# Two of the four parts of a state space's input weights formed in turned layout from tables, in place of 32 transposes

## The chip, the cores and the metric

One core of a Trainium2 chip runs the kernel. The metric is the device time of one execution in microseconds. The kernel before takes 1587.14 us, the median of three runs (1587.11 to 1588.02).

## What is computed

The reference is one layer of an encoder over two sequences of 512 tokens and width 1024, each with a memory of 256 rows, in float32. Three branches read the normalized input: a diagonal complex state space (32 groups of 16 channels, 64 states a group, run forwards and backwards), differential attention, and cross attention to the memory. Their outputs are gated, added and projected, and a feed-forward block follows. Cut to what the change touches:

```
h = rmsnorm(x) @ w_in;  u, q, k, v, xq, g = split(h)
mk, mv = split(rmsnorm(mem) @ w_mem_kv)          # keys and values of the memory
lam_bar = exp(lam * step)
b_bar = ((lam_bar - 1) / lam)[..., None] * b     # per group: 64 states x 16 channels
bu = einsum('lgh,gph->lgp', u, b_bar)
xs = scan(x_l = lam_bar * x_{l-1} + bu_l)        # once forwards, once backwards
y = real(einsum('lgp,ghp->lgh', xs, c))
```

## The kernel before

Eight tokens make a chunk. Within a chunk the state that u adds is a product with "input weights": for a group of 16 channels, a table of (8 tokens x 16 channels) by (2 directions x 64 states), real and imaginary, whose entry is lam_bar to a power q that depends on the token, times gamma = (lam_bar - 1) / lam, times b. The names: `pr`, `pi` are the powers of lam_bar (real, imaginary), `qr`, `qi` those in the tokens' order for the input, `xr_`, `xi_` for the output, `gr`, `gi` gamma, `b_r`, `b_i` b times gamma, `l8r`, `l8i` the eighth power for the scan. The 32 groups go in four parts `o` of eight.

`input_weights(o)` forms, for each part, two tables with states on the partitions (`cxr`, `cxi`, L1602 to L1611: six products or sums of 128x1024 on the vector engine, DVE). The matmul that uses them wants tokens and channels on the partitions, so TensorE (PE) turns each 128x128 piece (L1623), eight pieces to a table, and the scalar engine (ACT) copies them from PSUM to `wb` (L1624). The first three parts are formed ahead (L1628), the fourth later (L1693). L1687 multiplies `u_`, the projected input read back from DRAM in chunks (L1674), with `wb`.

All of this is a generator, `s5_gen`. The main function advances it at fixed places between the work on the memory, the input projection and the gates. There the rest of the code runs thus: a weight is loaded to `wf` on the SyncE queue (SP, L146), cast to `wh` on ACT (L134), and the rest `wl` is formed on DVE (L135); `wf`, `wh`, `wl` have two buffers each. The memory's values are four accumulating calls `mem_v(0)` to `mem_v(3)`, with the weights w_mv[0] to w_mv[3]; the four PSUM banks that they fill are emptied by ACT copies to `mf` (L368) and sent to DRAM (L373). The input projection follows, with w_in[0] and w_in[1] first, in the same four banks. `x_norm` (L252 to L254) makes the normalized input, `xh` and `xl`, in the same time, with a factor that PE turns into rows (L69 `rs`).

Each engine works through its own list in order. A scheduler sets the lists when the kernel is built, from its own view of times and the given ties (`issue_after`, `keep_in_program_order`); every instruction waits for its operands and buffers by semaphores. All loads named here are on SP's queue, which is in order as well, and the code of the generator shares the engines with everything else: an instruction that has to wait holds up what stands behind it on its engine.

Of the kernel before, what the change touches and what calls it, by code (L numbers as in the profile page):

```python
# [10 lines left out]
F32 = mybir.dt.float32  # L11
# [3 lines left out]
ALU = mybir.AluOpType  # L15
# [4 lines left out]
P = 128  # L20
# [11 lines left out]
G = 32  # L32
# [1435 lines left out]
def s5_gen(k):  # L1468

    tc, nc, a, slot, aux, drp, ident = k.tc, k.nc, k.a, k.slot, k.aux, k.drp, k.ident  # L1470
    V, S, PO, PE = nc.vector, nc.scalar, nc.gpsimd, nc.tensor
# [3 lines left out]
    cp = rt.enter_context(tc.tile_pool(name="s5c", bufs=1, side="right", reuse_waits="tile"))  # L1475
# [9 lines left out]
    def sm(nm, n=G):  # L1485
        return pp.tile([P, n], F32, tag="m_" + nm, name=nm)
# [40 lines left out]
    pr = pp.tile([P, 9, G], F32, name="pr")  # L1527
    pi = pp.tile([P, 9, G], F32, name="pi")
# [15 lines left out]
    ta, tb = (pp.tile([P, 512], F32, name=n_) for n_ in ("ta", "tb"))  # L1544
    t84a = ta[:, : 8 * G].rearrange("p (e g) -> p e g", g=G)
    t84b = tb[:, : 8 * G].rearrange("p (e g) -> p e g", g=G)
# [6 lines left out]
    mr, gr, gi, dn = sm("mr"), sm("gr"), sm("gi"), sm("dn")  # L1553
# [8 lines left out]
    V.tensor_tensor(out=gr, in0=gr, in1=dn, op=ALU.mult)  # L1562
    V.tensor_tensor(out=gi, in0=gi, in1=dn, op=ALU.mult)

    yield
    br, bi = pp.tile([P, G, 16], F32, name="br"), pp.tile([P, G, 16], F32, name="bi")
    cr, cn = cp.tile([P, G, 16], F32, name="cr"), cp.tile([P, G, 16], F32, name="cn")
    nc.sync.dma_start(br, a["b_re"])
# [8 lines left out]
    cmul(V, b_r, b_i, br, bi, gr.unsqueeze(2).broadcast_to(bs), gi.unsqueeze(2).broadcast_to(bs),  # L1577
         ta.rearrange("p (g h) -> p g h", h=16), tb.rearrange("p (g h) -> p g h", h=16))

    qr, qi = cp.tile([P, 8, G], F32, name="qr"), cp.tile([P, 8, G], F32, name="qi")  # L1580
    xr_, xi_ = cp.tile([P, 8, G], F32, name="xr_"), cp.tile([P, 8, G], F32, name="xi_")
    for (q_, x_, s_) in ((qr, xr_, pr), (qi, xi_, pi)):
        S.copy(q_[0:64], s_[0:64, 7::-1, :])
        S.copy(q_[64:128], s_[64:128, 0:8, :])
        S.copy(x_[0:64], s_[0:64, 1:9, :])
        S.copy(x_[64:128], s_[64:128, 8:0:-1, :])
    l8r = sp.tile([P, 2, G, NS], F32, name="l8r")
# [8 lines left out]
    def by_group(v, o):  # L1596
        return v[:, 8 * o : 8 * o + 8, :].unsqueeze(2).broadcast_to(sh4)

    def by_token(v, o):
        return v[:, :, 8 * o : 8 * o + 8].rearrange("p e g -> p g e").unsqueeze(3).broadcast_to(sh4)  # L1600

    def cprod(tag, ar, ai, xr, xi, sub):  # L1602


        tiles = [slot(tag, [P, 8, 8 if sub else 9, 16], name=n_) for n_ in ("cxr", "cxi")]
        for o_, x1, x2, op in ((tiles[0], ar, ai, ALU.subtract if sub else ALU.add), (tiles[1], ai, ar, ALU.add if sub else ALU.subtract)):
            o_ = o_[:, :, 0:8, :]
            t1 = slot(tag, sh4, name="ct1")
            V.tensor_tensor(out=t1, in0=x1, in1=xr, op=ALU.mult)
            V.tensor_tensor(out=o_, in0=x2, in1=xi, op=ALU.mult)  # L1610
            V.tensor_tensor(out=o_, in0=t1, in1=o_, op=op)  # L1611
        return tiles


    def input_weights(o):
        res = []
        for w_ in cprod("it", by_group(b_r, o), by_group(b_i, o), by_token(qr, o), by_token(qi, o), True):
            w_ = w_.rearrange("p g e h -> p (g e h)")
            t_ = slot("wb", [P, 8 * P], name="wb")
            for g4 in range(2):  # L1620
                tr = aux()
                for g in range(4):
                    PE.transpose(tr[:, g * P : (g + 1) * P], w_[:, (4 * g4 + g) * P : (4 * g4 + g + 1) * P], ident)  # L1623
                S.copy(t_[:, g4 * 512 : g4 * 512 + 512], tr)  # L1624
            res.append(t_)
        return res

    wbs = [input_weights(o) for o in range(3)]  # L1628
    yield

    gD = drp.tile([G, 16, 15, 16], F32, name="gD5")
    cD = drp.tile([4, 2, P, 8, 144], F32, name="cD")
# [5 lines left out]
    def output_weights(o):  # L1638
        Orf, Onf = cprod("it", by_group(cr, o), by_group(cn, o), by_token(xr_, o), by_token(xi_, o), False)
        PO.tensor_copy(Orf[:, :, 8, :], cr[:, 8 * o : 8 * o + 8, :])  # L1640
        PO.tensor_copy(Onf[:, :, 8, :], cn[:, 8 * o : 8 * o + 8, :])
        Orf, Onf = (o_.rearrange("p g e h -> p g (e h)") for o_ in (Orf, Onf))
        nc.sync.dma_start(cD[o, 0], Orf)
        nc.sync.dma_start(cD[o, 1], Onf)
        hs = slice(8 * o, 8 * o + 8)
        for ri, s_ in enumerate((b_r, b_i)):
            S.copy(l48[0:64, ri, :, 0:16], s_[0:64, hs, :])
            S.copy(l48[64:128, ri, :, 16:32], s_[64:128, hs, :])
            S.copy(l48[:, ri, :, 32:48], s_[:, hs, :])
        kps = [aux() for _ in range(2)]  # L1650
        for g4, kp in enumerate(kps):
            for g in range(2):
                for ri, o_ in ((1, Onf), (0, Orf)):
                    for hf in range(2):
                        tc.keep_in_program_order(
                            PE.matmul(kp[64 * hf : 64 * hf + 48, g * 144 : (g + 1) * 144], l48[:, ri, 4 * g4 + 2 * hf + g, :],
                                      o_[:, 4 * g4 + 2 * hf + g, :], start=(ri == 1), stop=(ri == 0)))
        for g4, kp in enumerate(kps):
            gk = cp.tile([112, 2, 144], F32, tag="gk", name="gk", bufs=2)
            for hf in range(2):  # L1660
                r0 = 64 * hf
                S.copy(gk[r0 : r0 + 48].rearrange("p g c -> p (g c)"), kp[r0 : r0 + 48, : 2 * 144])
                gv = gD[8 * o + 4 * g4 + 2 * hf : 8 * o + 4 * g4 + 2 * hf + 2].rearrange("g h t q -> h g (t q)")
                nc.sync.dma_start(gv[:, :, 128:240], gk[r0 : r0 + 16, :, 0:112])
                nc.sync.dma_start(gv[:, :, 0:112], gk[r0 + 16 : r0 + 32, :, 16:128])
                nc.sync.dma_start(gv[:, :, 112:128], gk[r0 + 32 : r0 + 48, :, 128:144])

    output_weights(0)
    output_weights(1)
    uv = k.uD.rearrange("(g h) j s c -> j h g (s c)", h=16)  # L1670
    u_ = slot("su", [P, G, NS * NC], name="u_")
# [27 lines left out]
    for i in range(2, NC):  # L1699
        p_ = sp.tile([P, 2, G * NS], F32, tag="p_", name="p_")  # L1700
        q_ = sp.tile([P, 2, G * NS], F32, tag="q_", name="q_")
# [29 lines left out]
    for o in range(4):  # L1731
# [4 lines left out]
        x2 = slot("x2", [P, 2, 8 * NS, NC], name="x2")  # L1736
# [24 lines left out]
def _tok(x):  # L1761

    return x.reshape(NC, T, *x.shape[1:]).swapaxes(0, 1).reshape(L, *x.shape[1:])
# [30 lines left out]
def layout(i):  # L1794
    i = {k_: np.asarray(v_) for k_, v_ in i.items()}
    a = {}
    x = np.stack([_tok(i["x_prompt"][0]), _tok(i["x_sample"][0])])
    a["xT"] = x.reshape(NS, L, KD, P).transpose(0, 3, 2, 1)
    mem = np.concatenate([i["mem_prompt"][0], i["mem_sample"][0]])
    a["xN"] = x.reshape(NS, 4, P, DM)  # L1800
    a["memN"] = mem.reshape(4, P, DM)
    a["memT"] = mem.reshape(2 * NMEM, KD, P).transpose(2, 1, 0)
    w = i["w_in"][0]
    a["w_in"] = _mtiles(w)
    a["w_v"] = np.stack([_moving(w[:, 1536 + 256 * h : 1792 + 256 * h], 4) for h in range(2)])
    wk = i["w_mem_kv"][0]
    a["w_mk"] = _mtiles(wk[:, :512])
    a["w_mv"] = _moving(wk[:, 512:], 2)
    a["w_glu"] = _mtiles(i["s5_w_glu"][0])
    a["w_up"] = np.stack([_mtiles(i["w_up"][0, n]) for n in range(3)])  # L1810
    a["w_out"] = _mtiles(i["w_out"][0])
    a["w_fg"] = _mtiles(i["w_ffn_in"][0][:, :FF])
    a["w_fu"] = _mtiles(i["w_ffn_in"][0][:, FF:])
    a["w_fo"] = _mtiles(i["w_ffn_out"][0])
    vecs = {"norm_mix": i["norm_mix"][0], "norm_mem": i["norm_mem"][0], "norm_ffn": i["norm_ffn"][0],
            "norm_final": i["norm_final"], "s5_d": i["s5_d"][0], "s5_b_glu": i["s5_b_glu"][0],
            "diff_subln": i["diff_subln"][0]}
    a["vecs"] = np.concatenate([_cols(vecs[n]) for n in VEC], axis=1)
    a["ident"] = np.eye(P, dtype=np.float32)
    a.update(_rope())  # L1820
    lam = np.stack([i["diff_lambda_q1"][0], i["diff_lambda_q2"][0], i["diff_lambda_k1"][0], i["diff_lambda_k2"][0]])
    a["lamv"] = np.broadcast_to(lam[None], (P, 4, 64))
    dpg = lambda v: v.transpose(0, 2, 1).reshape(P, G)
    a["lam_re"] = dpg(i["s5_lambda_re"][0])
    a["lam_im"] = dpg(i["s5_lambda_im"][0])
    a["log_step"] = dpg(np.broadcast_to(i["s5_log_step"][0][:, :, None], (2, G, 64)))
    for nm in ("re", "im"):
        b = i["s5_b_" + nm][0]
        a["b_" + nm] = b.transpose(0, 2, 1, 3).reshape(P, G, 16)
        c = i["s5_c_" + nm][0]  # L1830
        a["c_" + nm] = c.transpose(0, 3, 1, 2).reshape(P, G, 16)
    return {k_: np.ascontiguousarray(v_, dtype=np.float32) for k_, v_ in a.items()}
# [20 lines left out]
```

## Time and profile before

| What | us |
|---|---|
| median of three runs | 1587.14 |
| the profiled execution | 1586.94 |
| its span, first to last instruction | 1585.2 |
| PE busy (7738 matmuls and transposes) | 1574.0 |
| DVE busy | 1170.4 |
| ACT busy | 631.6 |
| all waits of PE for other engines | 5.1 |
| the 64 transposes of L1623 lie between | 74 and 131 |

A row of a timeline in the profile has the start in us, the length, the engine, the line and operation, what is written and read with partitions x elements, a count of like instructions, and in brackets the idle time before with what ended it. Matmuls are pipelined: a row's length is longer than the distance to the next. Rows of the view of one line have the shortest, median and longest duration in ns.

### The profile page before, as it was taken

The numbers are of one execution on the slowest core, as the hardware profiler recorded it, in microseconds if no ns is written. First come the engines' busy times: TensorE is split into PE (matmuls) and PEld (weight loads), VectorE is DVE, ScalarE is ACT, GpSimd is POOL, SyncE is SP. The second block draws the span as 40 slices with busy tenths as digits, with TensorE's granted clock in tenths as the row PEclk, the third lists the DMA queues.
The fourth block names the chain that finished last, engine by engine and source line by source line (L and its number), as shares of the span: only waits on it lengthen the run. The fifth ranks groups of instructions, "written<-read, shape, count | busy, mean of one in ns | idle before, by whom it ended". The sixth has DMA issues, their size and how long they took to land. (4 is left out here: it accounts for less than half of the span.)

```text
span 1585.2 us, 21351 instructions
## 1 busy us (share of the span) xinstructions
PE 1574.0 (99%) x7738; PEld 1310.4 (83%) x7738; DVE 1170.4 (74%) x1859; ACT 631.6 (40%) x1115; POOL 549.5 (35%) x434
## 2 busy tenths in 40 slices
PE   9999999999999999999999999999999999999998
PEld 7888888888898779778888888888888888888777
DVE  7978995076774776866545669788888877988864
ACT  6644223265552455564223443333333333233323
POOL 0010000001333321300343355767777553444663
PEclk9999999999999999999999999999999999999999
DMA  9553623676763121135544422333333323885412
GB/s 363 183 170 119 212 94 116 180 266 204 269 218 113 41 100 41 47 127 174 198 140 128 137 93 93 112 107 120 120 120 125 118 84 128 306 324 184 160 61 107
DMA packets 105675, 237.84 MB, mean 150 GB/s; under 512 B 13665, under 2 KB 45409, under 8 KB 105569
## 3 DMA queue, kind: packets, MB, share of 16 engines
q1 hardware_dynamic: 104992, 236.06, 44.2%
q8 instruction: 61, 1.00, 0.3%
q14 instruction: 46, 0.37, 0.1%
q10 hardware_dynamic: 576, 0.41, 0.1%
HBM read 165.16 MB, written 71.27 MB: 149 GB/s over the span
## 5 line engine op out<-in xcount | busy, mean ns | idle before, releaser
L66 PE MATMUL bkmm<-xh,wh 128*128 128x512 f32 x640 | 255.3, 399 | 0.0
L66 PE MATMUL bkmm<-xh,wl 128*128 128x512 f32 x640 | 250.6, 392 | 0.0
L66 PE MATMUL bkmm<-xl,wh 128*128 128x512 f32 x640 | 250.1, 391 | 0.0
L66 PE MATMUL bkmm<-tl,wh 128*128 128x512 f32 (+1 forms) x621 | 241.1, 388 | 0.0
L66 PE MATMUL bkmm<-th,wl 128*128 128x512 f32 (+1 forms) x621 | 240.7, 388 | 0.0
L66 PE MATMUL bkmm<-th,wh 128*128 128x512 f32 (+1 forms) x621 | 240.7, 388 | 0.0
L134 ACT CAST wh<-wf 128x1024 fp32r<-128x1024 f32 (+2 forms) x134 | 117.6, 878 | 261.2 <-PE bkmm L66 190.4
L135 DVE TENSOR_TENSOR wl<-wf,wh 128x1024 fp32r<-128x1024 f32 (+2 forms) x134 | 147.6, 1102 | 60.5 <-ACT wh L134 55.4
L66 PE MATMUL bkmm<-th,w 128*128 128x512 f32 x432 | 140.7, 391 | 1.9 <-DVE nsq L1112 1.2
L66 PEld LDWEIGHTS bkmm<-xh,wh 128*128 128x128 f32 x640 | 120.3, 188 | 26.2 <-issue 3.4
L66 PEld LDWEIGHTS bkmm<-xh,wl 128*128 128x128 f32 x640 | 120.2, 188 | 26.2 <-issue 0.4
L66 PEld LDWEIGHTS bkmm<-xl,wh 128*128 128x128 f32 x640 | 120.4, 188 | 22.3
L66 PEld LDWEIGHTS bkmm<-th,wh 128*128 128x128 f32 x621 | 116.6, 188 | 24.0
L66 PEld LDWEIGHTS bkmm<-th,wl 128*128 128x128 f32 x621 | 116.5, 188 | 24.1 <-DVE wl L135 0.2
L66 PEld LDWEIGHTS bkmm<-tl,wh 128*128 128x128 f32 x621 | 116.6, 188 | 23.8
L1175 POOL TENSOR_TENSOR up<-up,acc 128x512 f32<-128x512 f32 x44 | 83.7, 1920 | 90.6 <-DVE up L1112 86.8
L452 POOL TENSOR_TENSOR raw<-raw 128x128 f32<-128x128 f32 x28 | 14.6, 523 | 288.9 <-DVE nb L543 231.9
L66 PEld LDWEIGHTS bkmm<-th,w 128*128 128x128 f32 x432 | 80.9, 188 | 22.1 <-DVE nsq L1112 2.1
L792 POOL TENSOR_TENSOR mg<-mg,gl 128x1024 f32<-128x1024 f32 x16 | 43.8, 2740 | 136.8 <-DVE gl L788 132.1
L66 PE MATMUL bkmm<-tl,w 128*128 128x512 f32 x216 | 84.1, 389 | 0.0
L134 ACT CAST wh<-ws 128x1024 fp32r<-128x1024 f32 x44 | 46.3, 1052 | 91.3 <-PE bkmm L66 49.7
L66 PE MATMUL bkmm<-yh,wh 128*128 128x512 f32 x192 | 76.2, 397 | 0.0
(663 smaller groups left out, 3535.4 us busy)
## 6 DMA issues: line engine op xcount, KB each, us to landing
wf<-in_w_in SPq DMA_DIRECT2D x40, 512.0 KB, 3.9
wD<-hl SPq DMA_DIRECT2D x28, 512.0 KB, 2.9
w<-wD SPq DMA_DIRECT2D x28, 512.0 KB, 4.8
gD<-gt SPq DMA_DIRECT2D x24, 512.0 KB, 2.9
gl<-gD SPq DMA_DIRECT2D x24, 512.0 KB, 3.7
wf<-in_w_fg SPq DMA_DIRECT2D x22, 512.0 KB, 3.6
wf<-in_w_fu SPq DMA_DIRECT2D x22, 512.0 KB, 3.5
aD<-ac SPq DMA_DIRECT2D x22, 512.0 KB, 2.8
```

Of the source, the lines that this page charges most:

```text
L66: return self.put(self.eng.matmul(*args, **kw))
L134: h = S.copy(hi, src)
L135: l_ = V.tensor_tensor(out=lo, in0=src, in1=hi.bitcast(F32), op=ALU.subtract)
L452: PO.tensor_tensor(out=a22, in0=a21, in1=a22, op=ALU.add)
L792: PO.tensor_tensor(out=mg[m], in0=mg[m], in1=gt, op=ALU.add)
L1175: PO.tensor_tensor(out=up, in0=up, in1=accs[s], op=ALU.mult)
```

## The change

For parts 1 and 2 (the second and third) the input weights are formed with tokens and channels on the partitions at once. Tables in that layout are needed for both factors:

- The power times gamma, `qgr` and `qgi`, is formed for the 16 groups of both parts by six small DVE instructions (128x8x16, in the new code after L1563), in the scratch tiles `ta` and `tb`. PE turns both (two transposes, L1577), ACT copies them from PSUM back into `ta` (L1579), and two DMAs write them to DRAM as `qD` (L1581). The four ACT copies that make `qr` and `qi` move ahead to this place; before, they stood with those of `xr_` and `xi_` behind b times gamma.
- b in turned layout, `bt_re` and `bt_im`, comes as two new inputs, laid out on the host.
- `tables_in(o)` loads four tables of 128x1024 for a part: two of b (512 KB each, L1644) and two of the power, each by eight DMAs that read one row of 4 KB of `qD` into 16 partitions (L1647). They use four of the five slots `mem` that the memory's work holds until `mem_v` is through.
- `turned_weights` multiplies them by six DVE instructions of 128x1024 a part (L1656 to L1658), whose result is `wb` itself.

Part 1 stands with part 0, part 2 behind `output_weights(0)`. Parts 0 and 3 are as before. So 32 of the 64 transposes and eight of the 16 ACT copies go, two transposes, one ACT copy, six small DVE instructions and 38 DMAs come.

```diff
--- before.py
+++ after.py
@@ -1562,7 +1562,23 @@
     V.tensor_tensor(out=gr, in0=gr, in1=dn, op=ALU.mult)
     V.tensor_tensor(out=gi, in0=gi, in1=dn, op=ALU.mult)
 
+    qr, qi = cp.tile([P, 8, G], F32, name="qr"), cp.tile([P, 8, G], F32, name="qi")
+    for (q_, s_) in ((qr, pr), (qi, pi)):
+        S.copy(q_[0:64], s_[0:64, 7::-1, :])
+        S.copy(q_[64:128], s_[64:128, 0:8, :])
+    qgr, qgi = (t_[:, 8 * G : 12 * G].rearrange("p (e g) -> p e g", e=8) for t_ in (ta, tb))
+    qs_, mid = [P, 8, 16], slice(8, 24)
+    cmul(V, qgr, qgi, qr[:, :, mid], qi[:, :, mid], gr[:, mid].unsqueeze(1).broadcast_to(qs_),
+         gi[:, mid].unsqueeze(1).broadcast_to(qs_), t84a[:, :, :16], t84b[:, :, :16])
     yield
+    qD = drp.tile([2, 8, 16, P], F32, name="qD")
+    tr = aux()
+    for ri, q_ in enumerate((qgr, qgi)):
+        PE.transpose(tr[:, ri * P : (ri + 1) * P], q_.rearrange("p e g -> p (e g)"), ident)
+    qt = ta[:, : 2 * P].rearrange("p (a n) -> p a n", n=P)
+    S.copy(qt.rearrange("p a n -> p (a n)"), tr[:, : 2 * P])
+    for ri in range(2):
+        nc.sync.dma_start(qD[ri].rearrange("e g n -> (e g) n"), qt[:, ri])
     br, bi = pp.tile([P, G, 16], F32, name="br"), pp.tile([P, G, 16], F32, name="bi")
     cr, cn = cp.tile([P, G, 16], F32, name="cr"), cp.tile([P, G, 16], F32, name="cn")
     nc.sync.dma_start(br, a["b_re"])
@@ -1577,11 +1593,8 @@
     cmul(V, b_r, b_i, br, bi, gr.unsqueeze(2).broadcast_to(bs), gi.unsqueeze(2).broadcast_to(bs),
          ta.rearrange("p (g h) -> p g h", h=16), tb.rearrange("p (g h) -> p g h", h=16))
 
-    qr, qi = cp.tile([P, 8, G], F32, name="qr"), cp.tile([P, 8, G], F32, name="qi")
     xr_, xi_ = cp.tile([P, 8, G], F32, name="xr_"), cp.tile([P, 8, G], F32, name="xi_")
-    for (q_, x_, s_) in ((qr, xr_, pr), (qi, xi_, pi)):
-        S.copy(q_[0:64], s_[0:64, 7::-1, :])
-        S.copy(q_[64:128], s_[64:128, 0:8, :])
+    for (x_, s_) in ((xr_, pr), (xi_, pi)):
         S.copy(x_[0:64], s_[0:64, 1:9, :])
         S.copy(x_[64:128], s_[64:128, 8:0:-1, :])
     l8r = sp.tile([P, 2, G, NS], F32, name="l8r")
@@ -1625,8 +1638,29 @@
             res.append(t_)
         return res
 
-    wbs = [input_weights(o) for o in range(3)]
-    yield
+    def tables_in(o):
+        tabs = [slot("mem", [P, 8 * P], name="tab") for _ in range(4)]
+        for t_, nm in zip(tabs[2:], ("bt_re", "bt_im")):
+            nc.sync.dma_start(t_, a[nm][:, 8 * P * o : 8 * P * (o + 1)])
+        for ri, t_ in enumerate(tabs[:2]):
+            for e in range(8):
+                nc.sync.dma_start(t_[16 * e : 16 * e + 16],
+                                  qD[ri, e, 8 * o - 8 : 8 * o].rearrange("g n -> (g n)").unsqueeze(0).broadcast_to([16, 8 * P]))
+        return tabs
+
+    def turned_weights(q_r, q_i, bt_r, bt_i):
+        res = []
+        for x1, x2, op in ((bt_r, bt_i, ALU.subtract), (bt_i, bt_r, ALU.add)):
+            t_ = slot("wb", [P, 8 * P], name="wb")
+            t1 = slot("it", [P, 8, 9, 16], name="ct1").rearrange("p g e h -> p (g e h)")[:, : 8 * P]
+            V.tensor_tensor(out=t1, in0=x1, in1=q_r, op=ALU.mult)
+            V.tensor_tensor(out=t_, in0=x2, in1=q_i, op=ALU.mult)
+            V.tensor_tensor(out=t_, in0=t1, in1=t_, op=op)
+            res.append(t_)
+        return res
+
+    tab = tables_in(1)
+    wbs = [input_weights(0), turned_weights(*tab)]
 
     gD = drp.tile([G, 16, 15, 16], F32, name="gD5")
     cD = drp.tile([4, 2, P, 8, 144], F32, name="cD")
@@ -1666,6 +1700,9 @@
                 nc.sync.dma_start(gv[:, :, 112:128], gk[r0 + 32 : r0 + 48, :, 128:144])
 
     output_weights(0)
+    tab = tables_in(2)
+    wbs.append(turned_weights(*tab))
+    yield
     output_weights(1)
     uv = k.uD.rearrange("(g h) j s c -> j h g (s c)", h=16)
     u_ = slot("su", [P, G, NS * NC], name="u_")
@@ -1826,6 +1863,8 @@
     a["log_step"] = dpg(np.broadcast_to(i["s5_log_step"][0][:, :, None], (2, G, 64)))
     for nm in ("re", "im"):
         b = i["s5_b_" + nm][0]
+        bt = b.transpose(3, 1, 0, 2).reshape(1, 16, G * P)
+        a["bt_" + nm] = np.broadcast_to(bt, (8, 16, G * P)).reshape(P, G * P)
         a["b_" + nm] = b.transpose(0, 2, 1, 3).reshape(P, G, 16)
         c = i["s5_c_" + nm][0]
         a["c_" + nm] = c.transpose(0, 3, 1, 2).reshape(P, G, 16)
```

The lists of the engines change so. Lines are those of each kernel, so the same code has other numbers behind the new lines (L1585 before is L1598 after); `xt_147` and `xt_148` are first tiles of the two sequences' input, `wh<-wf` is the cast of a weight.

The first place is ACT from the last `xh` of the first sequence on; the three casts of weights there are w_mv[3], w_in[0] and w_in[1], in this order. Before:

```order
L253 CAST xh_130<-xt_147 128x512
L134 CAST wh<-wf 128x1024
L253 CAST xh_123<-xt_148 128x512
L253 CAST xh_124<-xt_148 128x512
L134 CAST wh<-wf 128x1024
L253 CAST xh_125<-xt_149 128x512
L253 CAST xh_126<-xt_149 128x512
L368 COPY mf<-bkmm 128x512 x2
L253 CAST xh_127<-xt_150 128x512
L134 CAST wh<-wf 128x1024
L1583 COPY qr<-pr 64x256
```

With the change, from the same row:

```order
L253 CAST xh_130<-xt_147 128x512
L1579 COPY ta<-bktr 128x256
L134 CAST wh<-wf 128x1024
L253 CAST xh_123<-xt_148 128x512
L253 CAST xh_124<-xt_148 128x512
L134 CAST wh<-wf 128x1024
L253 CAST xh_125<-xt_149 128x512
L253 CAST xh_126<-xt_149 128x512
L253 CAST xh_127<-xt_150 128x512
L134 CAST wh<-wf 128x1024
```

The copy of the new transposes has come in ahead of the cast of w_mv[3], and the two `mf` copies are no longer ahead of the cast of w_in[1]. They stand further down; these are the rows of the change from that cast on:

```order
L134 CAST wh<-wf 128x1024
L1598 COPY xr__735<-pr 64x256
L1599 COPY xr__735<-pr 64x256
L1598 COPY xi__736<-pi 64x256
L1599 COPY xi__736<-pi 64x256
L1604 COPY l8r<-pr 128x32 x2
L1605 ACTIVATE l8i<-pi 128x32
L368 COPY mf<-bkmm 128x512
L1606 COPY l8i<-pi 128x32
```

The first `mf` copy has moved behind the cast of w_in[1], four copies of `xr_` and `xi_` and three of the eighth power.

The second place is PE between `mem_v(2)` and `mem_v(3)` (`mh_142` and `ml_146` are the memory's tiles of `mem_v(3)`), as a piece of the difference:

```order
 L66 MATMUL bkmm<-wl,mh_141 128x512 x8
 L69 MATMUL bktr<-ident,rs 128x128 x4
+L1577 MATMUL bktr<-ident,ta 128x128
+L1577 MATMUL bktr<-ident,tb 128x128
 L66 MATMUL bkmm<-wh,mh_142 128x512 x2
 L66 MATMUL bkmm<-wh,ml_146 128x512 x2
```

The two new transposes stand directly ahead of `mem_v(3)`.

The third place is ACT some 25 rows earlier, in the first sequence's `xh` (the cast of a weight between is w_mv[1]). Before:

```order
L253 CAST xh_124<-xt_147 128x512
L134 CAST wh<-wf 128x1024
L238 ACTIVATE tk,ss<-tk 128x1024 x2
L253 CAST xh_125<-xt_147 128x512
L134 CAST wh<-wf 128x1024
```

With the change:

```order
L253 CAST xh_124<-xt_147 128x512
L1567 COPY qr<-pr 64x256
L1568 COPY qr<-pr 64x256
L134 CAST wh<-wf 128x1024
L1567 COPY qi<-pi 64x256
L1568 COPY qi<-pi 64x256
L238 ACTIVATE tk,ss<-tk 128x1024 x2
L253 CAST xh_125<-xt_147 128x512
L134 CAST wh<-wf 128x1024
```

The copies that make `qr` stand ahead of the cast of w_mv[1] now, those of `qi` ahead of the cast of w_mv[2].

## The prediction

> **What bounds the kernel now.** I read the page first: the span and the busy times.
>
> ```profile
> span 1585.2 us, 21351 instructions
> PE 1574.0 (99%) x7738; PEld 1310.4 (83%) x7738; DVE 1170.4 (74%) x1859; ACT 631.6 (40%) x1115; POOL 549.5 (35%) x434
> ```
>
> PE is busy in 99% of the span, every other engine far less. Then the waits of PE, by what ended them; I show the three longest.
>
> ```profile
> PE bkmm L66 <- DVE nsq L1112: 1.2, 2, 0.6
> PE bktr L66 <- DVE pad_r L82: 1.2, 1, 1.2
> PE bktr L66 <- ACT nsq L1417: 0.7, 1, 0.7
> ```
>
> All seven rows of that view come to 5.1 us. So the time is PE's own work, one instruction behind the other, and two rules follow. Work taken from PE shortens the span by its length. Whatever makes PE wait lengthens it by the whole wait, because there is no later idle time to swallow it. Work of DVE, ACT or the DMA queue counts only where PE comes to stand behind it. The places to look at are the 32 transposes that go, and the stretch from 34 to 60 us, where the change puts new instructions ahead of some on which PE waits.
>
> **Removed: 32 transposes, -3.54 us.** The line view of L1623, then PE's timeline around one group of eight.
>
> ```profile
> L1623 PE MATMUL bktr<-ident,cxr x32: 270/272/273, 74.3 to 126.9; 128*128 128x128 f32 x32
> L1623 PE MATMUL bktr<-ident,cxi x32: 272/272/273, 77.3 to 131.0; 128*128 128x128 f32 x32
> ```
> ```profile
> 74.08 0.40 PE L66 MATMUL bkmm<-xl,wh 128*128 128x512 f32 x1
> 74.32 1.03 PE L1623 MATMUL bktr<-ident,cxr 128*128 128x128 f32 x8
> 75.11 0.48 PE L66 MATMUL bkmm<-xh,wl 128*128 128x512 f32 x1
> 75.43 0.39 PE L66 MATMUL bkmm<-xh,wh 128*128 128x512 f32 x1
> 75.66 0.40 PE L66 MATMUL bkmm<-xl,wh 128*128 128x512 f32 x1
> ```
>
> The 272 ns of one is a duration in a pipeline, not its price. From the start of the group to the second matmul behind it are 75.43 - 74.32 = 1.11 us; without the group this holds one 128x512 matmul, whose pitch is 75.66 - 75.43 = 0.23. A group costs 0.88 to 0.89, and four groups go: 4 x 0.886 = **3.54 us**. The least that one could argue is the eight starts alone, 75.11 - 74.32 = 0.79, or 3.16. The eight ACT copies of L1624 that go as well free an engine at 40%: nothing.
>
> DVE forms as many 128x1024 products as before (six for each part), and six small ones more; that is weighed below.
>
> **Added ahead of the memory values' last weights: +2.03 us by the time PE starts on them.** Here are PE and ACT in the stretch where the order has changed (the order's rows are shown above).
>
> ```profile
> 36.38 1.98 PE L66 MATMUL bkmm<-wh,mh 128*128 128x512 f32 x8
> ...
> 47.37 0.60 PE L69 MATMUL bktr<-ident,rs 128*128 128x128 f32 x4
> 47.72 0.71 PE L66 MATMUL bkmm<-wh,mh 128*128 128x512 f32 x2
> ...
> 53.35 0.39 PE L66 MATMUL bkmm<-xh,wh 128*128 128x512 f32 x1
> ```
> ```profile
> 34.74 1.05 ACT L134 CAST wh<-wf 128x1024 fp32r<-128x1024 f32 x1
> ...
> 43.91 1.05 ACT L134 CAST wh<-wf 128x1024 fp32r<-128x1024 f32 x1
> ...
> 52.19 1.08 ACT L368 COPY mf<-bkmm 128x512 f32<-128x512 f32 x2
> ...
> 53.67 1.06 ACT L134 CAST wh<-wf 128x1024 fp32r<-128x1024 f32 x1
> 54.63 0.41 ACT L1583 COPY qr<-pr 64x256 f32<-64x256 f32 x1
> 55.04 0.40 ACT L1584 COPY qr<-pr 64x256 f32<-64x256 f32 x1
> ...
> 59.08 0.34 ACT L1591 COPY l8r<-pr 128x32 f32<-128x32 f32 x2
> 59.33 0.62 ACT L253 CAST xh<-xt 128x512 fp32r<-128x512 f32 x1
> 59.85 0.23 ACT L1592 ACTIVATE l8i<-pi 128x32 f32<-128x32 f32 x1
> 59.98 0.60 ACT L253 CAST xh<-xt 128x512 fp32r<-128x512 f32 x1
> ```
>
> First, the two qr copies now precede the cast at 34.74. They have starts 0.41 apart, and an ACT instruction of another kind starts some 0.1 before the end of the last, so two of them cost about 0.73. The cast ends 36.52 instead of 35.79; PE began at 36.38: **+0.2**.
>
> Second, DVE must finish six more small products before PE's two new transposes. This is its row of the nearest size and the subtraction (wl) that stands behind these products.
>
> ```profile
> 34.13 0.29 DVE L1541 TENSOR_TENSOR tb<-pi,pr 128x128 f32<-128x128 f32 x1
> 34.45 0.29 DVE L1542 TENSOR_TENSOR pi<-ta,tb 128x128 f32<-128x128 f32 x1
> ...
> 46.34 1.23 DVE L135 TENSOR_TENSOR wl<-wf,wh 128x1024 fp32r<-128x1024 f32 x1
> ```
>
> Six by 0.21 to 0.32 is 1.3 to 1.9; I take 1.3, as most of these are not in a chain with the one before. DVE waits 0.73 longer for the late cast, but does 0.4 of small work in that wait which it did later before. So tb is ready at 46.34 + 0.33 + 1.3 = 48.0. PE gets there at 47.37 + 0.2 + 4 x 0.0875 (the four L69 starts, 0.35 in all) + 0.09 = 48.0. I take 0.05 for this wait; its ends are 0 and 0.6.
>
> Third, and this is the step that costs: the ACT copy of these transposes now stands in ACT's order **ahead of the cast of the fourth memory-value weight** (43.91 above), and ACT works in order. That cast was done at 44.96, with 47.72 - 44.96 = 2.76 to spare. Now it waits for PE: transposes done at 48.05 + 0.27 = 48.3, copy of 128x256 about 0.4 (the trace has 0.40 for 64x256 and half of the 1.08 row, 0.54, for 128x512: those are the ends), cast 1.05, done at 49.75. PE, which must have it next, starts at 49.75 and not 47.72: **+2.03**, of which 1.6 is this wait and 0.2 the transposes themselves.
>
> **What that pushes: +3.16 more.** The subtraction that was at 46.34 follows the late cast, 49.75 to 50.98. It frees the raw weight buffer for the second input-projection weight, whose load SP issues then.
>
> ```profile
> 47.59 0.33 SPq L146 DMA_DIRECT2D wf<-in_w_in  x1
> ```
> ```profile
> DMA to landing us min/median/max: 3.9/3.9/3.9
> ```
>
> (The second view is L146 in that moment alone.) Before: issued 47.59, landed 51.5. After: issued 51.0, landed 54.9. ACT's order has the cast of that weight next (54.9 to 55.95), and then, unlike before, the four xr/xi copies (4 x 0.41), two l8r (0.25, from 59.08 to 59.33) and one l8i (0.13, 59.85 to 59.98), 2.0 together, **ahead of the first mf copy**. Before, two mf copies ran at 52.19, ahead of the cast. PE's first input-projection matmul (53.35) needs the bank that this copy empties. PE is through with the memory values at 49.75 + (53.35 - 47.72) = 55.38; the copy runs 57.95 to 58.54. **PE waits 3.16.** In all PE is then at 58.54 instead of 53.35, +5.19.
>
> I look for what is late next and find cover. In the order the later weights' casts keep their place against PE, and their loads shift with it. The first table products come on DVE behind the first part's, at 74 us and later; their last load can be issued by about 62 (16 x 0.47 behind the table write's landing at about 54), so they have ten microseconds. The 38 added DMAs are on SP, where nothing that PE needs within 5 us stands behind them except the two 512 KB tables ahead of the fourth memory-value weight; that load moves from 42.7 to about 45.2, hidden since its cast waits until 48.7.
>
> **Sum.** +5.19 - 3.54 = **+1.65 us**. Span 1585.2 + 1.65 = 1586.85; the profiled execution took 1586.94, 1.74 more than its span, so 1588.6; the median 1587.14 lies 0.20 above that execution: **1588.8 us**.
>
> **Rivals.**
>
> *The clock falls (slower).* The trace has PE at half rate in its first microseconds and again at the end.
>
> ```profile
> 1.18 4.63 PE L66 MATMUL bktr<-pad_r 128*128 128x128 f32 x20 [1.18 <-DVE pad_r L82]
> ```
> ```profile
> 1579.40:1585.00 5.60, 0.03 (x1) 0.00 (x0) 1.89 (x5) 0.37 (x1) 2.08 (x3) 0.50 0.69 241
> ```
>
> Twenty 128x128 matmuls in 4.63 are 0.22 apart, the transposes at 74.32 are 0.11 apart; behind 1579.4, where PE has nearly nothing to do, the granted clock is 0.50. Between 6 and 1579 us PE never paused over 0.7, so the trace does not show what a pause of 3.16 us at 55.4 does. If it lowers the clock, some 4.6 us of half rate follow, as at the start, and cost half of that: 1588.8 + 2.3 = **1591.1**. It decides if a pause somewhere between 0.7 and 3.16 us suffices. [...]
>
> *The table loads are slow (slower).* Each of the 32 reads one 4 KB row 16 times; none such is in the trace. Nearest are the u_ loads of the same 64 KB into 16 partitions: issue pace, time to landing, and bytes in a window where they alone land.
>
> ```profile
> 74.64 3.17 SPq L1674 DMA_DIRECT2D u__1192<-uD  x7
> ```
> ```profile
> DMA to landing us min/median/max: 2.1/2.9/5.1
> ```
> ```profile
> 106.20:107.30 1.10, 1.10 (x7) 0.89 (x6) 1.10 (x1) 1.03 (x4) 0.14 (x1) 1.00 0.75 286
> ```
>
> 3.17 / 7 = 0.45 to issue one, 64 KB at 286 GB/s = 0.23 to move it, so the issue sets the pace and 16 take 7.5 us. The third part's loads start only when the second part's products have read the four table slots, and are in at about 92, when DVE wants them at about 90: the first part's last product ends at 73.7 (first row below), the second part's products and a subtraction are five instructions of 1.2 us behind it and 1.65 later than before, so 81.5; 7.5 and a landing of 2.9 make 92, and seven more DVE instructions of 1.23 make 90. DVE's next wait (second row) gives 2.91 back.
>
> ```profile
> 72.47 1.22 DVE L1611 TENSOR_TENSOR cxi<-ct,cxi 128x1024 f32<-128x1024 f32 x1
> ...
> 103.45 1.23 DVE L135 TENSOR_TENSOR wl<-wf,wh 128x1024 fp32r<-128x1024 f32 x1 [2.91 <-ACT wh L134]
> ```
>
> So up to 0.9 us is spare there, 0.06 a load: from about 0.55 us a load each further 0.1 costs 1.6 us. At 1.0 the time is 1588.8 + 16 x 0.45 = **1596**; at 2.5, were sixteen reads of one row served one at a time, some 1620. Against it speaks that the row's 0.23 is half of the issue pace. [...]
>
> *The second wait is not there (same).* If the load lands earlier, or the bank is free otherwise, 3.16 goes: **1585.6**. The order of ACT speaks against it.
>
> *Both waits are small (faster).* Only the 0.2 + 0.2 of added work then stands against 3.54: **1584.0** or below. It needs the ACT copy not to hold the cast, which the order excludes, or removed transposes worth more than their starts.
>
> That the change doesn't do what it says is out: PE's order has 32 rows of L1623 fewer and two new.
>
> **How the numbers follow.** From no change a measurement here can tell about 0.2%, 3.2 us: 1584.0 to 1590.3. Forecast 57%, with a range of its own from 1587.0 to 1590.4 (the wait for tb to 0.6, the removed work down to 3.16, the load's landing 0.5 either way). Clock 19%, tables 9%, second wait absent 9%, both small 6%. Slower takes clock, tables and 3 of the forecast's tail: 0.31. Faster is both small and 2 of the second case: 0.08. Same: 0.61. The range goes from 1585.2 to 1591.8, which leaves out the tables beyond 0.7 us a load, and the fast end.
>
> **What would show it.** In the profile after: PE waiting about 1.6 us for ACT wh L134 near 48 us and about 3.2 for ACT mf L368 near 55; the first input-projection matmul at 58.5; PE 1.65 us later than before at 135 us, with the four groups gone; the clock 1.0 behind the second wait. If PE waits on DVE's table products near 90 us or later, the table loads are slow. If PE is at 53.4 with the input projection, my reading of ACT's order is wrong.

## The result, and the profile after

The changed kernel takes 1593.58 us (median of 6 runs, 1592.24 to 1595.97), the kernel before 1587.32 in the same runs: ratio 1.0039, 95% interval 1.0029 to 1.005, **6.3 us slower**. The forecast was 1588.8, with a range up to 1591.8. The profiled execution took 1595.0, span 1593.2, 8.0 more than the span of before.

The page after, its first two lines:

```profile
span 1593.2 us, 21338 instructions
PE 1574.7 (99%) x7708; PEld 1309.1 (82%) x7708; DVE 1171.5 (74%) x1865; ACT 626.7 (39%) x1108; POOL 549.2 (34%) x434
```

PE has 30 instructions less and yet the same busy time, which already says that some of them ran slower. The waits of PE after, the first three rows:

```profile
PE bkmm L66 <- ACT mf L368: 4.5, 1, 4.5
PE bkmm L66 <- ACT wh L134: 1.7, 2, 1.4
PE bkmm L66 <- DVE nsq L1112: 1.2, 2, 0.6
```

The two waits of the prediction head the list. PE's timeline after, at the same places as shown of before:

```profile
36.97 2.12 PE L66 MATMUL bkmm<-wh,mh 128*128 128x512 f32 x8 [0.28 <-ACT wh L134]
...
48.09 0.60 PE L69 MATMUL bktr<-ident,rs 128*128 128x128 f32 x4
48.53 0.27 PE L1577 MATMUL bktr<-ident,ta 128*128 128x128 f32 x1
48.72 0.33 PE L1577 MATMUL bktr<-ident,tb 128*128 128x128 f32 x1
50.45 0.74 PE L66 MATMUL bkmm<-wh,mh 128*128 128x512 f32 x2 [1.41 <-ACT wh L134]
...
60.82 0.79 PE L66 MATMUL bkmm<-xh,wh 128*128 128x512 f32 x1 [4.51 <-ACT mf L368]
61.41 0.63 PE L66 MATMUL bkmm<-xl,wh 128*128 128x512 f32 x1
61.84 0.63 PE L66 MATMUL bkmm<-xh,wl 128*128 128x512 f32 x1
```

Read the starts against those of before: 36.97 for 36.38, 50.45 for 47.72, 60.82 for 53.35, so PE is 0.6, 2.7 and 7.5 us late. Then look at the last rows: the same 128x512 matmuls that took 0.39, 0.23 apart, take 0.63, 0.43 apart. The clock has fallen; the windows of after say for how long (the last columns are the granted clock, the DMA share and GB/s):

```profile
59.50:66.10 6.60, 5.28 (x12) 4.13 (x13) 6.60 (x12) 4.86 (x16) 0.00 (x0) 0.50 0.66 200
66.30:68.00 1.70, 1.70 (x9) 1.38 (x8) 1.70 (x3) 0.00 (x0) 0.00 (x0) 1.00 1.02 357
```

When it is up again PE is 10.04 late; here are the row of before and the same matmul after:

```profile
58.90 0.39 PE L66 MATMUL bkmm<-xh,wh 128*128 128x512 f32 x1
```
```profile
68.94 0.39 PE L66 MATMUL bkmm<-xh,wh 128*128 128x512 f32 x1
```

So the slow clock cost 10.04 - 7.47 = 2.6. Behind the removed transposes the lag is 7.3 (178.27 for 171.01; it stays there up to 1350 us), and small late waits bring it to 7.9 at the end. In sum: 0.6 up to 37 us (0.15 of it was there at 35 us already, ahead of the first moved row, 34.71 for 34.56; the late cast adds 0.44 from start to start, of which 0.28 counts as idle), 2.1 for the two transposes and the first wait, 4.7 for the second wait, 2.6 for the clock, 2.8 back, 0.7 late.

The ACT rows behind the two waits, after:

```profile
49.08 0.37 ACT L1579 COPY ta<-bktr 128x256 f32<-128x256 f32 x1 [3.64 <-PE bktr L1577]
49.35 1.05 ACT L134 CAST wh<-wf 128x1024 fp32r<-128x1024 f32 x1
...
57.22 1.04 ACT L134 CAST wh<-wf 128x1024 fp32r<-128x1024 f32 x1 [1.09 <-DMA wf<-in_w_in]
58.17 0.40 ACT L1598 COPY xr__735<-pr 64x256 f32<-64x256 f32 x1
...
60.20 0.56 ACT L368 COPY mf<-bkmm 128x512 f32<-128x512 f32 x1
```

The copy waits 3.64 for PE with the cast behind it, and the first mf copy comes at 60.20, behind the cast at 57.22, which waited for its load. That load (SP's row and its landing):

```profile
51.69 0.33 SPq L146 DMA_DIRECT2D wf<-in_w_in  x1
```
```profile
DMA to landing us min/median/max: 5.4/5.4/5.4
```

### The profile page after: what moved, and what is told of

Its sections match the earlier page's. It is cut to its first block, busy times and chain, and to the rows that moved or that the text cites. A ratio compares the mean times of both kernels' runs of the same rounds, so it can differ in the third digit from the quotient of the medians.

```text
span 1593.2 us, 21338 instructions
## 1 busy us (share of the span) xinstructions
PE 1574.7 (99%) x7708; PEld 1309.1 (82%) x7708; DVE 1171.5 (74%) x1865; ACT 626.7 (39%) x1108; POOL 549.2 (34%) x434
## 5 line engine op out<-in xcount | busy, mean ns | idle before, releaser
L135 DVE TENSOR_TENSOR wl<-wf,wh 128x1024 fp32r<-128x1024 f32 (+2 forms) x134 | 153.0, 1142 | 63.5 <-ACT wh L134 59.1
```

What stands on the lines that cost most here:

```text
L135: l_ = V.tensor_tensor(out=lo, in0=src, in1=hi.bitcast(F32), op=ALU.subtract)
```

## The experiments

Theory one: the order of the lists on ACT makes PE wait, and the pause lowers the clock. Theory two: the added DMAs are what makes things late, or the transposes were worth little. All medians stand against the kernel before in the same runs (1587.46 to 1587.57).

**The transposes alone.** The kernel before, parts 1 and 2 without transposes and copies.

```diff
-    wbs = [input_weights(o) for o in range(3)]
+    wbs = [input_weights(0), unturned(1), unturned(2)]
```

`unturned` writes the products to `wb` directly, so what this kernel leaves out is the turning, and its input weights for these parts are not those of the reference.

> The kernel before with the 32 transposes of the second and third part and their eight ACT copies left out and nothing in their place (the products go to the matmuls unturned, so those parts of the input weights are not what the reference wants). Theory one, which says that removed transposes are worth their place in PE's row and the added waits ate it: 3.5 us faster than before, 1583.8, and no new wait on PE. Theory two, which says that transposes are partly hidden in the pipeline and were worth little from the start: within 1 us of before, 1586.5 or more.

Measured: 1585.85 (1584.26 to 1587.29), ratio 0.9988, 0.998 to 0.9997: 1.7 faster, between the theories. The profile shows both. The same row of the program stands at 170.10 in before and at 166.65 here:

```profile
170.10 0.39 PE L66 MATMUL bkmm<-xh,wh 128*128 128x512 f32 x1
```
```profile
166.65 0.50 PE L66 MATMUL bkmm<-xh,wh 128*128 128x512 f32 x1
```

PE is 3.45 ahead here. Of this, 0.44 was there before the first removed transpose (34.12 for 34.56), and one wait that before has not fell into their stage:

```profile
PE bktr L1700 <- DVE st L1704: 0.5, 1, 0.5
```

So this run alone shows some 3.0 to 3.5 for the 32 transposes. In the six changed kernels below that have no wait of PE in this stage (all but the one with the copies on GpSimd), PE's lag behind before shrank by 3.63 to 3.67 between 60 and 171 us of before. The price of 3.54 that was worked out fits. Later part of it goes in waits that before has not, the longest in this profile:

```profile
1351.88 0.50 PE L66 MATMUL bkmm<-th,w 128*128 128x512 f32 x1 [1.15 <-DVE u L1112]
```

DVE, which PE waits for here, had itself waited for a load 12 us earlier; before has none at this place:

```profile
1339.50 0.69 DVE L981 TENSOR_TENSOR ts<-fb,fa 128x512 f32<-128x512 f32 x1 [2.13 <-DMA fb<-aD]
```

**All 64 transposes**, to see whether a larger lead is lost too.

```diff
-    wbs = [input_weights(o) for o in range(3)]
+    wbs = [unturned(o) for o in range(3)]
...
-            wbs.append(input_weights(3))
+            wbs.append(unturned(3))
```

> The kernel before with all 64 transposes and their 16 ACT copies left out (the products of all four parts go to the matmuls unturned, so the input weights are not what the reference wants). The run without 32 of them was 3.45 us ahead at 170 us of its profile and 1.7 us at the end by the median. Theory A (what is given back are single small waits late in the program that hit now this run, now that, some 1 to 2 us in all, however large the lead): 1587.5 - 7.0 + 1.7 = 1582.2. Theory B (a later stage is bound by another engine or the DMA, so that a lead over 2 us is lost there whatever its size): 1585.3 or more, with one wait on PE of 3 us or more late in the profile.

Measured: 1583.44, ratio 0.9975, 0.9965 to 0.9985: 4.0 faster. Theory B falls (no wait of 3 us, no floor at 1585). Theory A holds in kind; in size more is given back, some 3 of 7, by several waits of under 0.6, such as

```profile
PE bkmm L66 <- ACT wh L134: 0.5, 1, 0.5
PE bkmm L66 <- DMA w<-wD: 0.5, 1, 0.5
PE bkmm L66 <- DVE gl L788: 0.4, 1, 0.4
```

**The mf copies ahead of the state space's copies** in the changed kernel.

```diff
-                S.copy(mfs[s][:, j], ob[2 * s + j])
+                last_mf = S.copy(mfs[s][:, j], ob[2 * s + j])
...
-    with yielding(last_s):
+    with yielding(last_s), tc.issue_after(last_mf.ins):
         next(s5)
```

> The changed kernel with one tie: the copies of xr, xi and the eighth power are issued behind the four mf copies, not ahead of them. The cast of the second input-projection weight stays ahead. Theory one (the second wait is ACT's order): the wait for mf falls from 4.5 us to about 2.5 (the load lands near 57.2, the cast takes 1.05, the first mf copy 0.56, PE is ready at 56.3); if the clock then stays up the time is 1593.6 - 2.0 - 2.4 = 1589.2, if it falls all the same 1591.6. Theory two (the added DMAs on the queue make what PE needs late): the wait stays above 4 us and the time above 1592.5.

Measured: 1590.49, ratio 1.0016, 1.0007 to 1.0025, 3.1 less than the changed kernel, and 1.3 more than expected with the clock up. Its first two waits and its clock:

```profile
PE bkmm L66 <- ACT mf L368: 1.7, 1, 1.7
PE bkmm L66 <- ACT wh L134: 1.6, 2, 1.4
```
```profile
57.60:60.60 3.00, 3.00 (x13) 2.51 (x14) 3.00 (x6) 2.95 (x8) 0.00 (x0) 1.00 0.96 254
```

The second wait fell further than expected, since the load took 4.6 here, and the clock stayed up in the profiled run (one profile does not say whether it did in the others). The first wait is untouched. Theory two falls for this wait: the DMAs are the same.

**The cast ahead of the copy**, alone.

```diff
     mw.append(weight(a["w_mv"][3]))
+    s_mv3 = last_s
...
-    with queued():
+    with queued(), tc.issue_after(s_mv3[0].ins):
         next(s5)
```

> The changed kernel with another single tie: the ACT copy of the two new transposes is issued behind the cast of the fourth memory-value weight, not ahead of it. Theory one: PE's first wait (1.4 us for the cast) goes, the second input-projection weight is issued some 1.8 us earlier, at about 49.9, PE is 1.4 earlier, so the second wait keeps about 4 us and the clock falls all the same: 1593.6 - 1.8 = 1591.8. Theory two: that weight's load lands late for the two 512 KB tables ahead of it, the cast waits for the load, and the first wait stays over 1 us: above 1592.8.

Measured: 1591.28, ratio 1.0021, 1.0012 to 1.003. The first wait is gone (0.2 is left, of the qr copies), the second one is 3.8 and the clock falls, as expected; the row is

```profile
PE bkmm L66 <- ACT mf L369: 3.8, 1, 3.8
```

**Both ties.**

> Both ties together. Theory one: no first wait; the second input-projection weight is issued near 49.9 and lands between 53.8 and 55.3, its cast and one mf copy end between 55.4 and 56.9, PE is ready near 54.9: a second wait of 0.5 to 2.0 us, no loss of clock: 1593.6 - 1.4 - 3.3 - 2.4 = 1586.5, give or take 0.8. Theory two: two waits of together over 4 us and above 1590.

Measured: 1588.76 (1587.3 to 1590.61), ratio 1.0006, 0.9997 to 1.0015. The two waits in question are as expected (0.2 and 1.8), but the time is 2.3 above the expectation. The profiled run shows two reasons. One is a late wait near 776 us, which before has not:

```profile
PE bkmm L66 <- DVE gl L789: 1.6, 1, 1.6
```

The other is the clock: the pause of 1.8 us lowered it, and PE's lag grew by 1.6 in the stretch at half.

```profile
53.25:56.65 3.40, 1.63 (x8) 1.02 (x7) 3.40 (x6) 3.05 (x6) 0.00 (x0) 1.00 0.99 280
56.70:60.00 3.30, 3.30 (x9) 2.56 (x9) 3.30 (x6) 3.25 (x12) 0.00 (x0) 0.50 0.67 196
60.10:62.00 1.90, 1.90 (x10) 1.56 (x9) 1.90 (x5) 1.90 (x7) 0.00 (x0) 1.00 1.03 330
```

**One part of the order in the kernel before**: the block with the mf copies and their two writes is written below the last `next(s5)` of that stretch; nothing else.

```diff
-    with tc.issue_after(last_s[0].ins):
-        mfs = []
...
     with yielding(last_s):
         next(s5)
+    with tc.issue_after(last_s[0].ins):
+        mfs = []
...
```

> The kernel before with one part of the new order alone: the mf copies are written behind the state space's copies in the code, so that on ACT they follow the cast of the second input-projection weight, the copies of qr, qi, xr, xi and the eighth power, and two casts of xh. No tables, no new transposes, no added DMA. Theory one (the order on ACT is what costs): the first mf copy waits for the second of these casts, which ends at 60.6 in the profile before, so PE waits for it from 53.4 to about 61.2, some 7.5 us, and the clock falls for 2.4 to 2.8 more: 1597.5. Theory two (without the added DMAs the order costs little): under 1590.

Measured: 1595.85 (4 runs, 1595.69 to 1596.26), ratio 1.0053, 1.0039 to 1.0066: 8.4 slower, without a table or an added DMA. The wait is 5.9 (the two casts of xh came earlier than in before), and the clock is at half for the rest of it and beyond:

```profile
PE bkmm L66 <- ACT mf L373: 5.9, 1, 5.9
```
```profile
57.10:63.70 6.60, 3.83 (x9) 3.09 (x10) 6.57 (x11) 5.18 (x18) 0.00 (x0) 0.50 0.52 187
63.90:66.00 2.10, 2.10 (x11) 1.72 (x10) 2.10 (x3) 0.20 (x1) 0.00 (x0) 1.00 0.31 125
```

This shows theory one by itself: an order on ACT that puts the mf copies behind is enough for a cost of this size. It isn't the very order of the changed kernel: the qr and qi copies and two casts stand ahead of the mf copies too.

**Why the order came about.** In both ties above the cast of w_in[1] still stands ahead of the mf copies. My reading is that the scheduler has its own view of time, in which the two 512 KB tables, issued ahead of the load of w_mv[3], make everything behind that load later. So one tie puts the table loads behind the load of w_in[1].

```diff
-    with yielding(last_s):
+    with yielding(last_s), tc.issue_after(last_w.ins):
         next(s5)
```

> The changed kernel with one tie of another sort: the table loads are issued behind the load of the second input-projection weight, so that the two 512 KB tables no longer stand on the queue ahead of the fourth memory-value weight. The scheduler's lists then put the ACT copy behind the casts and an mf copy ahead of the second input-projection weight's cast, as before. Theory one (ACT's order is the cost): the waits of 1.4 and 4.5 us go, the clock stays: before 1587.4 - 3.5 for the transposes + 0.5 for the qr copies and the two transposes + up to 1.5 given back late, as in the run without transposes: 1584.4 to 1585.9. Theory three (the load itself is slower now, 4.6 to 5.4 us instead of 3.9, for the writes and tables around it): a wait on PE of 1 us or more near 54 us is left, 1587 or more.

Measured: 1586.05 (1584.8 to 1587.71), ratio 0.9992, 0.9983 to 1.0001; **7.5 us less than the changed kernel by one tie**. ACT's rows of this kernel:

```profile
50.81 1.05 ACT L134 CAST wh<-wf 128x1024 fp32r<-128x1024 f32 x1
51.77 0.61 ACT L253 CAST xh<-xt 128x512 fp32r<-128x512 f32 x1
52.28 0.36 ACT L1579 COPY ta<-bktr 128x256 f32<-128x256 f32 x1
52.55 0.59 ACT L368 COPY mf<-bkmm 128x512 f32<-128x512 f32 x1
53.03 0.63 ACT L253 CAST xh<-xt 128x512 fp32r<-128x512 f32 x1
54.79 1.05 ACT L134 CAST wh<-wf 128x1024 fp32r<-128x1024 f32 x1 [1.13 <-DMA wf<-in_w_in]
```

The copy is behind the casts, an mf copy ahead of the cast of w_in[1], and that cast waits for the same slow load (5.7) without holding anything up: PE waits 0.3. It is faster than before by 1.5 in the medians, 0.15 above the range that was expected, with an interval that reaches no change. The run shows that the place of the table loads sets the order of ACT; the scheduler's own times were not looked at. This is the best that the change came to here.

**All three ties**, to see whether ACT's ties add something.

> Both ties on ACT's order and the tie of the table loads together. Theory one: as with the table loads tied alone, since the order of ACT is mended by either: within 0.7 us of that run, 1584.4 to 1585.9. If mf copies ahead of the cast are worth something more, up to 0.5 us less.

Measured: 1586.21, ratio 0.9992, 0.9983 to 1.0: the same as with the tables tied alone. Its profile has the late wait of 1.6 for DVE gl as well.

**The writes of the power table on ACT's queue**, with the first two ties, to find out why the load of w_in[1] is slow.

```diff
-        nc.sync.dma_start(qD[ri].rearrange("e g n -> (e g) n"), qt[:, ri])
+        nc.scalar.dma_start(qD[ri].rearrange("e g n -> (e g) n"), qt[:, ri])
```

> The kernel with both ties, and the two writes of the turned power table issued from ACT's queue, not from SyncE's behind the load of the second input-projection weight. If these writes slow that load (4.7 us with both ties, 3.9 before), it lands in 4.0 or less, the second wait falls by 0.7 to about 1.0 and the time by 0.7, or 2 and more if the clock then stays up: 1586.2. If the backlog of the two tables ahead of it does it, the landing stays at 4.6 or more and the time at 1588.7.

Measured: 1588.06 (1586.17 to 1592.38), ratio 1.0005, 0.9997 to 1.0014. The load took 5.2:

```profile
DMA to landing us min/median/max: 5.2/5.2/5.2
```

The landing is as in the second expectation, but the run doesn't settle the cause: from ACT's queue the writes went out at 48.78, just ahead of the load at 49.04, so they were still under way beside it (after, the same writes landed 5.0 and 5.3 us behind their issue). The kernel with the tables tied behind settles more. Its writes were issued 4.9 us behind this load, when a load of 3.9 would have landed, and it took 5.7; so the writes are not its cause. A backlog of weight loads isn't either: the load before it had landed 2 us earlier there. With all three ties the two tables as well were issued 3.7 us behind the load, and it took 5.4.

**The qr and qi copies on GpSimd**, with all three ties.

```diff
-        S.copy(q_[0:64], s_[0:64, 7::-1, :])
-        S.copy(q_[64:128], s_[64:128, 0:8, :])
+        PO.tensor_copy(q_[0:64], s_[0:64, 7::-1, :])
+        PO.tensor_copy(q_[64:128], s_[64:128, 0:8, :])
```

> All ties as in the kernel above and the four copies of qr and qi on GpSimd, which is idle there, not on ACT ahead of casts. Theory one: the last added wait of PE (0.28 us near 37 us for the cast behind the qr copies) goes: 0.2 to 0.3 us less than the kernel above, 1584.1 to 1585.6, and faster than before. Rival: the tables are late now, because the write of the power table stands behind the mf writes on the queue; then DVE waits over 4 us for them near 75 us and PE over 1 us behind it, and the time is 1587 or more.

Measured: 1587.69 (1585.2 to 1593.18), ratio 1.0004, 0.9995 to 1.0012. Neither expectation in full: the wait at 37 us is gone; DVE stands idle for 5.1 us ahead of a product of the second tables at 96.57, but PE waits for nothing behind that. The time is in the rival's range all the same, as DVE is late with other things, for which PE waits:

```profile
PE bkmm L66 <- DVE wl L135: 1.0, 1, 1.0
...
PE bktr L1578 <- DVE ta L1540: 0.4, 1, 0.4
```

Another list, other small waits, no gain.

## Why the prediction failed, point by point

- **Bound by PE, any wait counts in full:** right. It holds for every kernel above, with one addition: a gain does not count in full. Without 32 transposes PE had gained 3.0 to 3.5 us behind their stage, and the run was 1.7 faster at the end; the prediction let all of it arrive.
- **Removed, -3.54:** right as the price of the transposes (3.63 to 3.67 in the six kernels without a wait in their stage). In the changed kernel 2.8 came back, since PE lost some of it in that stage again, in a wait of 0.3 for ACT among others; the prediction put such losses at nothing.
- **qr copies, +0.2; tb, 0.05; first wait, 1.6:** 0.28, about 0.1 and 1.41 as idle time, so the mechanism is right. By the starts PE was 2.73 late ahead of `mem_v(3)`, not 2.03: the two copies put the cast 0.84 back on ACT and not 0.73 (35.03 to 35.87), which was 0.29 late already (34.52 for 34.23).
- **Second wait, 3.16:** the mechanism is right, row by row, and the kernel with one part of the order alone shows it by itself. The size is off: 4.51 idle, 4.74 by the starts. The term that was mis-sized is the load of w_in[1], taken at 3.9 us and measured at 5.4. In the four profiles without tables it took 3.5 to 3.9, in the eight with them 4.6 to 5.7. Neither the writes behind it, nor the weight load ahead of it, nor the place of the tables on the queue explains that; its cause stays open.
- **The clock:** the step that failed is the choice among the cases, by which the sum has nothing for the clock. The rival "the clock falls" had 19% and a price of 2.3; it is what happened, at 2.6. It was weighed by the length of one pause, 3.16, against a threshold of length that no run shows, so the low chance was my estimate. The true pause was 4.5; one of 1.8 lowered the clock as well, and one of 1.9 did not (last section). By the windows of the last section (3.41 us each, a fall behind 1.64 of PE busy or less), and if a pause is as likely to lie anywhere on their grid, 3.16 us leave at least 1.77 idle in one window unless the line between two windows falls into the middle 0.38 us of the pause: an estimate of eight cases in nine for the fall. So the low chance was wrong with either length.
- With the measured terms the sum closes: 0.6 + 2.1 + 4.7 + 2.6 - 2.8 + 0.7 = 7.9, for 8.0 in the profiled execution. Against the forecast of 1.65 the clock makes 2.6 of the difference, the second wait 1.6, the lag ahead of it 0.7, the losses in the transposes' stage 0.8 and the late waits 0.7. The median of the runs is 6.3 above before; their spread of 3.7 us may come from a pause that varies with the load, which is not shown.
- **Table loads:** right, they are hidden. DVE waits for them once, and PE never behind it:

```profile
DVE wb L1657 <- DMA tab<-qD: 2.7, 1, 2.7
```

- **One table load alone:** its time is not shown; the 1.0 and 2.5 us of the rival were assumed. Seven of them were issued in 3.31 us (row below), 0.47 apart, and the first landed 4.4 us after its issue, the fifth and sixth 3.4 and 3.1, so the landings kept up with the issue. But each goes into another 16 partitions and up to seven were under way at once, so the rate of one alone can't be read from them. The same holds for the 286 GB/s from which the prediction took 0.23 us a load.

```profile
57.42 3.31 SPq L1647 DMA_DIRECT2D tab<-qD  x7
```

- **What I looked past:** I read the new order as given, and didn't ask what set it. Two loads that PE never waits for stood ahead of one on the queue, and they moved rows on ACT, by my reading through the scheduler's estimate.

## What to carry to other kernels

On an engine that works in order, look for the first instruction of the new list that waits for the bound engine, and at what stands behind it; a copy of 0.37 us cost 1.4 that way, and 2.0 of the 4.5 were four copies of 0.4 and three smaller ones. Where a scheduler sets the lists, a transfer moved ahead can change rows on engines that have nothing to do with it: tie it, and read the lists again. Where a pause can leave the matmul engine idle for about half of one of the 3.41 us windows of the next section (1.77 with both ties), add the price of a clock at half (1.6 to 2.6 us here), and do not count a gain in one stage as a gain at the end before the waits behind it are seen.

## What the runs showed of the hardware

By the trace's records the clock was at half for 3.41 us with both ties (56.65 to 60.07) and with the cast first (58.78 to 62.20), and for 6.83, twice that, after (59.42 to 66.25) and with the mf copies behind (56.96 to 63.78). The stretch at full clock ahead of the fall in after is a whole multiple of it too: 54.61 us (4.81 to 59.42) are 16 of them. So the clock changed on a grid of windows of 3.41 us here, and the grid does not start with the pause (after, PE was idle from 56.31). No window had to be idle throughout for the fall: with both ties PE was busy 1.63 of the 3.40 us ahead of the fall, in which the pause took 1.8.

What counted in these runs is how a pause lies on the grid. Three windows of it, the first with both ties, the other two with the writes on ACT's queue:

```profile
773.45:776.86 3.41, 1.80 (x8) 1.23 (x7) 2.46 (x4) 1.53 (x2) 0.00 (x0) 1.00 0.14 16
```
```profile
51.32:54.73 3.41, 2.61 (x12) 1.76 (x10) 3.41 (x6) 2.61 (x5) 0.00 (x0) 1.00 1.03 383
54.73:58.15 3.42, 2.28 (x10) 1.90 (x11) 3.42 (x6) 3.40 (x8) 0.00 (x0) 1.00 0.54 137
```

The clock stayed up behind all three. The last two share a pause of 1.9, longer than the 1.8 that lowered the clock: the line between them cuts it into 0.80 and 1.14. The pause of 1.7 with the mf copies first was cut likewise (PE busy 2.37 and 2.80). Over these pauses the clock fell behind each window with PE busy 1.64 us or less (0.30 after, 0.64 with the cast first, 0.48 with the mf copies behind, 1.64 with both ties) and stayed up with 1.80 or more. Once at half, a window with 2.02 (after, 59.42 to 62.84) did not bring it back. Where between 1.64 and 1.80 the clock falls is not settled, and busy time doesn't sort the kernel's last microseconds: before, the clock fell at 1579.31 behind a window with 2.09.
